# Matrix memory: two gate tiles in the heads' stage, gate steps later; the rotary key's parts in one tile; the first halves' last squares added on VectorE

## The chip, the cores and the metric

The kernel runs on one core of one Trainium2 chip. The metric is the device time of one execution in microseconds (us); lower is better. Three executions of the kernel before took 2184.15, 2185.90 and 2186.45 us, median 2185.9 us.

## What is computed

A trunk of four residual layers over 1024 tokens of 1024 channels: latent attention, a gated MLP with a causal convolution, an mLSTM matrix memory, and a second gated MLP; each is normed (RMS) and modulated by a conditioning vector, and a last norm closes. The parts that matter here:

```
def mla_mixer(h, cos, sin, w_in, q_norm, w_q_up, kv_norm, w_kv_up, w_out):
    proj = h @ w_in                                   # 1024 -> 512 + 256 + 64
    cq, ckv, k_rope = jnp.split(proj, [MLA_Q_LORA, MLA_Q_LORA + MLA_KV_LORA], axis=-1)
    q = (rms_norm(cq, q_norm) @ w_q_up).reshape(B, S, MLA_HEADS, MLA_NOPE + MLA_ROPE)
    k_rope = apply_rope(k_rope, cos, sin)
    kv = (rms_norm(ckv, kv_norm) @ w_kv_up).reshape(B, S, MLA_HEADS, MLA_NOPE + MLA_V)
...
def mlstm_mixer(h, w_in, b_gates, head_norm, w_out):
    proj = h @ w_in
    q, k, v, o, gates = jnp.split(proj, [qk_w, 2 * qk_w, 2 * qk_w + v_w, 2 * qk_w + 2 * v_w], axis=-1)
    def step(carry, inp):                             # one chunk of 64 tokens, per head
        C, n, m = carry
...
        num = (inter_w[..., None] * jnp.einsum('bhvd,bhtd->bhtv', C, qt)
               + jnp.einsum('bhts,bhsv->bhtv', s_mat, vt))
...
        C_new = decay[..., None, None] * C + jnp.einsum('bhs,bhsv,bhsd->bhvd', ws, vt, kt)
        return (C_new, n_new, m_new), h_out
...
    y = hs.reshape(B, S, v_w) * jax.nn.sigmoid(o.astype(jnp.float32))
```

`o` are the output gates, eight tiles of 128 channels.

## The kernel before

**Form of a product.** Tokens lie along the free dimension in two halves of 512 (`hf`), channels along partitions. Each operand is split into a high and a low part in a reduced format (ScalarE copies the high part, VectorE subtracts for the low), and a product is `mm3` (L173): three matmuls of 128x512, high by high, high by low, low by high. The parts `hi` and `lo` of a weight come from `unit` (L164), which loads a raw tile and splits it; the raw tiles of the heads' stage rotate through a small number of buffers, so a load waits for the split of an earlier one. `mm3` also counts down a queue: `later(n, fn, key)` (L188) puts a step after n more calls of `mm3` in the program. Numbers for this stand in a table (L41 to L56). A scheduler then fixes the order on each engine; every engine, and SyncE (SP), which issues the loads and stores, works in that order.

**Start, about 0 to 125 us.** `in_k` (L352) multiplies the k-th 128 channels of both halves with seven weight tiles, for k of 0 to 7, into seven accumulators `ia`. Six tiles are the latent query and key/value; the seventh holds the 64 columns of the rotary key twice (the load is 896 columns wide), since its rotated partner is needed too. After the last k, `evac` (L443) scales the accumulators by the token's norm (`rbs`), `in_norms` (L503) squares and sums them (`ev`), `rstd_cols` (L245) sums over partitions with one-column matmuls (`st`), VectorE and GpSimd make `var` and `rstd`, a transpose spreads it (`rb`), and `norm_gain` (L493) makes `cqn` and `ckvn`, for which the products `qrp`, `kp` and `qp` wait. `rope_key` (L508) adds a bias on ScalarE, and rotates the key.

**Sums of squares.** `Squares.add` (L234) squares a tile on ScalarE and adds it on VectorE; `keep` (L228) squares only, and leaves the tile to the one-column matmuls as a second term. The last tile of a half is kept.

**Products of the memory, about 1126 to 1262 us.** `mixer_products` computes pairs of projection tiles with seven products in place of eight (a scheme after Strassen, over halves of tokens and channels), 4 `mm3` of 128x512 each: four pairs of q and k, two pairs of output gates (`PAIRS`, L88, `OG`, L89). Results go to memory, and the heads' stage loads them again (`ogd`, `qkd`).

**Heads' stage, about 1262 to 1447 us.** First the gate values: `gates0` to `gates3` (L1674 to L1731) are small steps on VectorE, ScalarE and TensorE (`gg`, `gr`, `gp`, `gcol`), put after 2, 18, 22 and 26 `mm3` of `ogates` (L1506), whose matmuls `inp` make the remaining output gates from tile OG on. The rows of the gates are stored (`gd`) and loaded again as rows of all partitions (`crow`, `ib`). Then for each of four heads: `prep` makes scores (`st`), transposed keys (`kp`) and their weighted split (`kw`); `chain` (L1568) runs eight chunks: `pc` is the update of state C, `po` the output from the chunk (`po<-va`) and from C (`po<-C`); `finish` transposes (`yT`). Between the chunks one `mm3` of `ogates` is put (L1764), between the chains the next head's values (`vp`). VectorE's queue holds the dot products of the modulation (`mraw`), the splits and C, in the scheduler's order.

Of the kernel before, what the change touches and what calls it, by code (L numbers as in the profile page):

```python
# [11 lines left out]
F32 = mybir.dt.float32  # L12
# [6 lines left out]
P = 128  # L19
D = 1024  # L20
S = 1024
KT = D // P
HS = 512
NH = 8
# [18 lines left out]
WARM = 14  # L43
W0, W0_RSTD, WF, WF_RSTD = (6, 10), (4, 3), (4, 5), (4, 4)
SHARE = 7
GATES = (2, 18, 22, 26)
MODS = (0,) * 4 + (2,) * 11 + (3,)
# [39 lines left out]
U_MV0 = (U_MV, U_MV + 1, U_MG)  # L87
PAIRS = tuple((U_MQ + i, U_MK + i) for i in range(4)) + ((U_MO, U_MO + 1), (U_MO + 2, U_MO + 3))  # L88
OG = 4  # L89

# [9 lines left out]
def trunk_kernel(ctx: ExitStack, tc: tile.TileContext, xT, pos, c_d, cols_d, mod_w, win, winT, w0, w1, wf, wd, out):  # L100
# [72 lines left out]
    def mm3(ps, ls, rs, first, last, more=False):  # L173

        lh, ll = ls
        rh, rl = rs
        pe.matmul(ps, lh, rh, start=first, stop=False, skip_group_check=more)  # L177
        pe.matmul(ps[:, 0:rl.shape[-1]], lh, rl, start=False, stop=False, skip_group_check=more)  # L178
        pe.matmul(ps, ll, rh, start=False, stop=last, skip_group_check=more)  # L179
        for e in list(queue):  # L180
            e[0] -= 1
            if e[0] == 0:
                queue.remove(e)
                e[1]()


# [131 lines left out]
    sraw = block(4, [P, 4, D], F32, "sraw")  # L318
    wraw = block(5, [P, 4, 896], F32, "wraw")
    us = [[(p0w if k < INNER else p0).tile([P, 896], F32R, name=f"win{j}{k}") for j in "hl"] for k in range(KT)]  # L320

# [14 lines left out]
    def prepare(k):  # L336
        hi, lo = us[k]
        raw = wraw[:, k % 4, :]
        mod_dot(0, 8 + k, sraw[:, k % 4, :])
        mod_bias(0, 8 + k)  # L340
        act.activation(hi, raw, AF.Copy)
        scaled(0, k)
        dve.tensor_tensor(lo, raw, hi.bitcast(F32), ALU.subtract)

# [7 lines left out]
    def in_k(acc, k, hf, then=None):  # L352

        for m in range(7):
            mm3(acc[m], wk(us[k], m), halves(h, hf, k), k == 0, k == KT - 1)
            if then:
                then(m)
# [145 lines left out]
    def in_norms(hf, raw, ev, ps):  # L503

        sq = [Squares(ev, bufs=4), Squares(ev, bufs=4)]
        for m in range(6):
            sq[m // 4].add(raw[:, m, :], bias=inb[:, m:m + 1])
        def rope_key():  # L508
            sl = slice(hf * HS, (hf + 1) * HS)
            t = raw[:, 6, :]  # L510
            act.activation(t, t, AF.Identity, bias=inb[:, 6:7])
            rope_apply(t, raw[:, 7, :], hf)
            act.activation(kkh[:, sl], t, AF.Copy)
            dve.tensor_tensor(kkl[:, sl], t, kkh[:, sl].bitcast(F32), ALU.subtract)

        if hf == 0:
            rope_key()
        cqn[hf] = block(2 + 2 * hf, [P, 2, 4, HS], F32R, "cqn")
        if hf == 0:
            ckvn[0] = block(3, [P, 2, 2, 2, HS], F32R, "ckvn")  # L520

        def gain_q(rb):
            if hf == 1:
                t = p_a[:, 6 * HS:7 * HS]
                act.activation(t, rb, AF.Copy)
                rb = t
            with tc.high_priority():
                norm_gain(raw[:, 0:4], inb[:, 0:4], rb, 4, "qn", cqn[hf][:, 0], cqn[hf][:, 1])

        def gain_kv(rb):  # L530
            if hf == 1:
                t = p_a[:, 7 * HS:8 * HS]
                act.activation(t, rb, AF.Copy)
                rb = t
            norm_gain(raw[:, 4:6], inb[:, 4:6], rb, 2, "kvn", ckvn[0][:, hf, 0], ckvn[0][:, hf, 1])
            if hf == 1:
                rope_key()

        rstd_later(sq[0], 512, cqn[hf], gain_q, EVAC[0], ps)
        rstd_later(sq[1], 256, cqn[hf], gain_kv, EVAC[1], ps)  # L540
# [331 lines left out]
    def out_proj(px, psC, osrc, us, w, l, early=0):  # L872
# [7 lines left out]
        for hf in range(2):  # L880
# [3 lines left out]
            for m in range(KT):  # L884
# [6 lines left out]
                store_x(2 * l, hf, m, x)  # L891
                ssq.keep(x[:, m, :]) if m == KT - 1 else ssq.add(x[:, m, :])
            if hf == 0:
# [76 lines left out]
    def mlp(px, psC, T, l, u_d, pd, done, cols, extra=None, scaled=None, store=None, more=None):  # L970
# [238 lines left out]
        def d_run(i, p, w, t0=0, width=HS):  # L1209
# [14 lines left out]
            if g == len(DG) - 1 and op in ("B22", "T3", "B21", "T4"):  # L1224
                for c0, cw_ in ((0, HS),) if hf == 0 else cols:
                    if t0 <= c0 < t0 + width:
# [3 lines left out]
                        with tc.high_priority():  # L1230
                            if op in ("T3", "T4") and (p == 3 or p == 2 and c0 > 0):
                                stats[hf, c0].keep(xs[hf][:, m, c0:c0 + cw_])
# [272 lines left out]

    def ogates():  # L1506
        for m in range(OG, KT):
            u = unit(w1[U_MO + m])
            for hf in range(2):
# [123 lines left out]
    def run(gen):  # L1633
        while True:
            try:
# [11 lines left out]
                     lambda: pm.tile([P, D], F32, tag="mraw", bufs=MRAWS, name=nm("mraw")), crow2)  # L1647
    va = va_tiles()
    v0 = wp.tile([P, 1024], F32, tag="wraw", bufs=wraws, name=nm("v0"))
    nc.sync.dma_start(v0, va_d)  # L1650
# [82 lines left out]
    for n, gate_step in zip(GATES, (gates0, gates1, gates2, gates3)):  # L1733
        later(n, gate_step, gcol)
    og = ogates()
    piece(og, GATES[3] + 1)
# [8 lines left out]
    for hd in range(MH):  # L1745
# [17 lines left out]
        for _ in chain(hd, pre, va, obs):  # L1763
            piece(og)  # L1764
        ends = lambda hd=hd, obs=obs: finish(hd, obs, 1)
# [56 lines left out]
def arrange(inputs):  # L1822
# [24 lines left out]
    wi = a["mla_w_in"][0]  # L1847
    win = np.concatenate([wi, wi[:, 768:]], axis=1).reshape(KT, P, 896)
    winT = np.ascontiguousarray(win.reshape(D, 896).T).reshape(7, P, D)

# [55 lines left out]
```

## Time and profile before

| | us |
|---|---|
| median of three executions | 2185.9 |
| profiled execution, its own time | 2185.47 |
| its span, first to last instruction | 2183.5 |
| TensorE busy in the span | 2149.2 (98%) |
| VectorE busy | 1746.4 (80%) |
| ScalarE busy | 1076.8 (49%) |
| mean granted TensorE clock | 0.994 |

In the rows of a profile PE is TensorE, PEld its loading of weights, DVE VectorE, ACT ScalarE, POOL GpSimd, SPq the queue of SyncE. A row of instructions gives its start, its length, the engine, the line of the kernel, the operation, the tile written and those read, their shape, how many follow each other, and in brackets the idle time before and what ended it. A row of a stretch gives its ends, its length, then for each engine busy time and (x) instructions, the granted clock of TensorE (1.00 is full), the share of the DMA engines that was busy, and GB/s. Matmuls overlap, so a row's length is not its price: spacing is.

### The profile page before, as it was taken

How to read it: one execution, taken by the hardware profiler on the slowest of the kernel's cores; microseconds unless marked ns; L12 is line 12 of the kernel's file. 1: busy time of each engine (PE TensorE's matmuls, PEld its weight loads, DVE VectorE, ACT ScalarE, POOL GpSimd, SP SyncE). 2: the span in 40 equal slices, each digit the busy share in tenths (PEclk: the TensorE clock that was granted, in tenths of full speed). 3: DMA queues.
4: the chain of work that ended last, by engine and by line, in shares of the span. 5: the costliest groups of instructions: out<-in, count | busy, mean ns of one | idle time of the engine just before them, and what ended most of it. 6: DMA issues, size and time to landing. Idle time of an engine off the chain costs nothing.

```text
span 2183.5 us, 28611 instructions
## 1 busy us (share of the span) xinstructions
PE 2149.2 (98%) x10485; PEld 1804.2 (83%) x10485; DVE 1746.4 (80%) x2789; ACT 1076.8 (49%) x1794; POOL 53.0 (2%) x136
## 2 busy tenths in 40 slices
PE   9999999999999999999999999999999999999998
PEld 7878888787888888878888879988888888887887
DVE  8877778659878777899988458886886777779997
ACT  6465566446544444443365464454554444453335
POOL 0000000000000000000000001000000000000000
PEclk9999999999999999999999999999999999999999
DMA  8412334842443342643143454474143332246212
GB/s 319 151 52 58 98 101 151 272 136 67 160 139 129 127 130 97 204 161 103 51 172 131 142 182 151 147 262 142 59 145 102 111 121 92 78 157 216 68 52 77
DMA packets 120588, 289.89 MB, mean 133 GB/s; under 512 B 13376, under 2 KB 21120, under 8 KB 120448
## 3 DMA queue, kind: packets, MB, share of 16 engines
q1 hardware_dynamic: 120048, 287.68, 40.1%
q8 instruction: 82, 1.34, 0.3%
q14 instruction: 58, 0.48, 0.1%
q10 hardware_dynamic: 400, 0.39, 0.1%
HBM read 233.07 MB, written 52.33 MB: 131 GB/s over the span
## 4 chain that ended last, share of the span: by engine, by line
PE 84%; DVE 7%; DMA 4%; ACT 3%; issue 1%; SPq 1%; POOL 1%; DVEq 0%; POOLq 0%; ACTq 0%
PE pa L179 7%; PE pa L177 7%; PE pa L178 7%; PE pd L179 3%; PE da L177 3%; PE da L178 3%; PE da L179 3%; PE pd L177 3%; PE pd L178 3%; PE sc L675 3%; PE op L177 2%; PE op L179 2%; PE op L178 2%; PE db L179 2%; PE db L177 2%; PE db L178 2%
## 5 line engine op out<-in xcount | busy, mean ns | idle before, releaser
L177 PE MATMUL pa<-T,whi 128*128 128x512 f32 x528 | 205.9, 390 | 0.0
L178 PE MATMUL pa<-T,whi 128*128 128x512 f32 x528 | 205.5, 389 | 0.0
L179 PE MATMUL pa<-T,wlo 128*128 128x512 f32 x528 | 205.1, 389 | 0.0
L993 ACT ACTIVATE whi<-wsum 128x512 fp32r<-128x512 f32 x200 | 121.9, 625 | 145.4 <-PE pa L178 61.5
L994 DVE TENSOR_TENSOR wlo<-wsum,whi 128x512 fp32r<-128x512 f32 x200 | 134.4, 686 | 40.9 <-ACT whi L993 39.6
L993 ACT ACTIVATE whi<-raw 128x512 fp32r<-128x512 f32 x150 | 90.7, 624 | 123.3 <-PE pb L178 61.0
L178 PE MATMUL da<-U,whi 128*128 128x512 f32 (+1 forms) x364 | 139.1, 382 | 0.0
L177 PE MATMUL da<-U,whi 128*128 128x512 f32 (+1 forms) x364 | 139.1, 382 | 0.0
L179 PE MATMUL da<-U,wlo 128*128 128x512 f32 (+1 forms) x364 | 138.7, 382 | 0.0
L994 DVE TENSOR_TENSOR wlo<-raw,whi 128x512 fp32r<-128x512 f32 x150 | 101.6, 686 | 33.2 <-ACT whi L993 33.2
L1197 ACT ACTIVATE whi<-raw 128x1024 fp32r<-128x1024 f32 (+1 forms) x60 | 59.2, 987 | 131.0 <-PE da L178 50.0
L177 PEld LDWEIGHTS pa<-T,whi 128*128 128x128 f32 x528 | 99.1, 188 | 22.4 <-ACT whi L993 1.2
L179 PEld LDWEIGHTS pa<-T,wlo 128*128 128x128 f32 x528 | 99.1, 188 | 20.6
L178 PEld LDWEIGHTS pa<-T,whi 128*128 128x128 f32 x528 | 99.1, 188 | 20.2
L1038 ACT ACTIVATE ct<-a,cols 128x512 f32<-128x512 f32 x88 | 70.8, 809 | 84.1 <-DVE a L1060 47.8
L177 PE MATMUL db<-U,whi 128*128 128x512 f32 x264 | 103.4, 392 | 0.8 <-ACT whi L1197 0.8
L179 PE MATMUL db<-U,wlo 128*128 128x512 f32 x264 | 102.7, 390 | 1.5 <-DVE wlo L1198 1.5
L1148 ACT ACTIVATE U<-q 128x1024 fp32r<-128x1024 f32 x84 | 80.0, 980 | 48.6 <-DVE q L1147 22.8
L178 PE MATMUL db<-U,whi 128*128 128x512 f32 x264 | 102.8, 390 | 0.0
L169 ACT ACTIVATE whi<-wraw 128x1024 fp32r<-128x1024 f32 x58 | 60.9, 1056 | 84.0 <-PE op L178 61.1
L177 PE MATMUL op<-oh,whi 128*128 128x512 f32 x256 | 99.9, 392 | 0.9 <-ACT oh L729 0.9
L178 PE MATMUL op<-ol,whi 128*128 128x512 f32 x256 | 99.6, 390 | 0.0
(432 smaller groups left out, 6176.1 us busy)
## 6 DMA issues: line engine op xcount, KB each, us to landing
raw<-in_wf SPq DMA_DIRECT2D x96, 512.0 KB, 3.9
wraw<-in_w SPq DMA_DIRECT2D x58, 512.0 KB, 3.7
mraw<-in_mod_w SPq DMA_DIRECT2D x56, 512.0 KB, 3.7
ud<-ct SPq DMA_DIRECT2D x88, 256.0 KB, 2.2
q<-ud SPq DMA_DIRECT2D x88, 256.0 KB, 4.7
raw<-in_wd SPq DMA_DIRECT2D x32, 512.0 KB, 3.9
pa<-in_mod_w SPq DMA_DIRECT2D x24, 512.0 KB, 3.6
x<-xd SPq DMA_DIRECT2D x48, 256.0 KB, 4.5
```

The source lines that it names most:

```text
L169: act.activation(hi, raw, AF.Copy)
L177: pe.matmul(ps, lh, rh, start=first, stop=False, skip_group_check=more)
L178: pe.matmul(ps[:, 0:rl.shape[-1]], lh, rl, start=False, stop=False, skip_group_check=more)
L179: pe.matmul(ps, ll, rh, start=False, stop=last, skip_group_check=more)
L675: pe.matmul(ps[:, cs], a[:, qs if n < 3 else qrs_], b[:, cs], start=n == 0, stop=n == 4)
L993: act.activation(hi, src, AF.Copy)
L994: eng.tensor_tensor(lo, src, hi.bitcast(F32), ALU.subtract)
L1038: act.activation(t, a[:, 2:], AF.Identity, bias=col(f"cb{l}", m), scale=cw(m, 2))
L1148: act.activation(hi, w, AF.Copy)
L1197: act.activation(hi, src, AF.Copy)
```

## The change

1. **Rotary key in one tile.** The weights are loaded 832 columns wide, and the low part of the key's 64 columns is written beside its high part, so one tile holds [high | low]. `mm2` does one full matmul with that tile and one with its first 64 columns and the low half of the tokens' values: two in place of three. The accumulator's upper 64 rows are then a part that has to be added; `rope_key` moves the halves past each other with two transfers of 64x512 and adds them and the bias on VectorE, where ScalarE had added the bias.
2. **One pair of output gates less** among the products, and two tiles more in `ogates`, two `mm3` between chunks instead of one; the first of its weights is loaded ahead.
3. **Gate steps** after 2, 20, 24, 28 `mm3`; `rb` of the second half's norm before the memory after 8 instead of 3.
4. **Last squares** of the first half are added on VectorE at both output projections and both MLPs; only the second half's are kept.

```
-W0, W0_RSTD, WF, WF_RSTD = (6, 10), (4, 3), (4, 5), (4, 4)
+W0, W0_RSTD, WF, WF_RSTD = (6, 10), (4, 8), (4, 5), (4, 4)
-GATES = (2, 18, 22, 26)
+GATES = (2, 20, 24, 28)
-PAIRS = tuple((U_MQ + i, U_MK + i) for i in range(4)) + ((U_MO, U_MO + 1), (U_MO + 2, U_MO + 3))
-OG = 4
+PAIRS = tuple((U_MQ + i, U_MK + i) for i in range(4)) + ((U_MO, U_MO + 1),)
+OG = 2
...
+    def mm2(ps, u, rs, first, last):
+
+        rh, rl = rs
+        both = lambda: pe.matmul(ps, u, rh, start=first, stop=last)
+        if first:
+            both()
+        pe.matmul(ps[0:64, :], u[:, 0:64], rl, start=False, stop=False)
+        if not first:
+            both()
+        turns()
...
-        act.activation(hi, raw, AF.Copy)
+        act.activation(hi[:, 0:WIN], raw, AF.Copy)
         scaled(0, k)
-        dve.tensor_tensor(lo, raw, hi.bitcast(F32), ALU.subtract)
+        for o, c0, c1 in ((lo, 0, 768), (hi[:, WIN:896], 768, WIN)):
+            dve.tensor_tensor(o, raw[:, c0:c1], hi[:, c0:c1].bitcast(F32), ALU.subtract)
...
-            t = raw[:, 6, :]
-            act.activation(t, t, AF.Identity, bias=inb[:, 6:7])
-            rope_apply(t, raw[:, 7, :], hf)
+            t, rot = raw[:, 6, :], raw[:, 7, :]
+            for a, b in ((0, 64), (64, 0)):
+                nc.sync.dma_start(rot[a:a + 64, :], t[b:b + 64, :])
+            dve.scalar_tensor_tensor(t, t, inb[:, 6:7], rot, ALU.add, ALU.add)
+            rope_apply(t, rot, hf)
...
-                ssq.keep(x[:, m, :]) if m == KT - 1 else ssq.add(x[:, m, :])
+                ssq.keep(x[:, m, :]) if hf and m == KT - 1 else ssq.add(x[:, m, :])
...
-                            if op in ("T3", "T4") and (p == 3 or p == 2 and c0 > 0):
+                            if op == "T4" and (p == 3 or p == 2 and c0 > 0):
...
-            piece(og)
+            piece(og, 2)
```

TensorE, start, first k: `ia_180` is the seventh accumulator before, `ia_181` with the change, `winh` and `winl` the high and low weights, `h_94` and `h_95` the high and low values. Before:

```order
L177 MATMUL ia_180<-h_94,winh_98 128x512
L178 MATMUL ia_180<-h_95,winh_98 128x512
L179 MATMUL ia_180<-h_94,winl_99 128x512
L177 MATMUL ia_174<-h_94,winh_100 128x512
L178 MATMUL ia_174<-h_95,winh_100 128x512
```

And now:

```order
L194 MATMUL ia_181<-h_94,winh_98 128x512
L197 MATMUL ia_181<-h_95,winh_98 64x512
L178 MATMUL ia_175<-h_94,winh_100 128x512
L179 MATMUL ia_175<-h_95,winh_100 128x512
L180 MATMUL ia_175<-h_94,winl_101 128x512
```

The third matmul is gone, and the second writes 64 rows.

VectorE, end of the start stage: from the additions of the squares of the second half (`ev`) to its gains (`raw<-raw,inb,pa`); `wlo` is a weight's low part, `k` and `q` are splits of products. Before:

```order
L243 TENSOR_TENSOR ev_874<-ev_874 128x512
L607 TENSOR_TENSOR k_938<-kp_939,k_937 128x512
L256 TENSOR_SCALAR var_959<-st_954 128x4
L256 TENSOR_SCALAR var_974<-st_969 128x4
L610 SCALAR_TENSOR_TENSOR q_949<-qp_950,q_948 128x512
L170 TENSOR_TENSOR wlo_1545<-wraw_1542,whi_1544 128x1024
L496 SCALAR_TENSOR_TENSOR raw_843<-raw_843,inb,pa_908 128x512 x3
```

And now:

```order
L630 TENSOR_TENSOR k_932<-kp_933,k_931 128x512
L259 TENSOR_TENSOR ev_868<-ev_868 128x512
L633 SCALAR_TENSOR_TENSOR q_943<-qp_944,q_942 128x512
L272 TENSOR_SCALAR var_953<-st_948 128x4
L272 TENSOR_SCALAR var_968<-st_963 128x4
L534 SCALAR_TENSOR_TENSOR raw_838<-raw_838,inb 128x512
L171 TENSOR_TENSOR wlo_1541<-wraw_1538,whi_1540 128x1024
L517 SCALAR_TENSOR_TENSOR raw_838<-raw_838,inb,pa_902 128x512 x3
```

The key's split now stands ahead of the last addition, the query's split ahead of `var`, and the new addition of the rotary key between `var` and the gains.

VectorE, heads' stage, from `gcol` to the first head's last `kw`. Before:

```order
L1729 COPY gcol<-gcol_11227 128x128
L610 SCALAR_TENSOR_TENSOR kw_11269<-kp_11255,gcol,kw_11268 128x128 x2
L1544 TENSOR_SCALAR crow<-crow,gcol 128x128 x4
L610 SCALAR_TENSOR_TENSOR kw_11269<-kp_11255,gcol,kw_11268 128x128
L1554 TENSOR_TENSOR qT_10934<-qT_10934,ib_11233 128x512
L1544 TENSOR_SCALAR crow<-crow,gcol 128x128
L610 SCALAR_TENSOR_TENSOR kw_11269<-kp_11255,gcol,kw_11268 128x128
L1553 TENSOR_TENSOR crow<-crow,st_11248 128x512
```

And now:

```order
L1757 COPY gcol<-gcol_11076 128x128
L633 SCALAR_TENSOR_TENSOR kw_11118<-kp_11104,gcol,kw_11117 128x128 x3
L1570 TENSOR_SCALAR crow<-crow,gcol 128x128 x4
L171 TENSOR_TENSOR wlo_11817<-wraw_11814,whi_11816 128x1024
L1580 TENSOR_TENSOR qT_10781<-qT_10781,ib_11082 128x512
L1579 TENSOR_TENSOR crow<-crow,st_11097 128x512
L633 SCALAR_TENSOR_TENSOR kw_11118<-kp_11104,gcol,kw_11117 128x128
```

Three of the four `kw` now stand ahead of the rows of the gates, and the fourth behind a weight's split, `qT` and the product with the scores. On TensorE ten `inp` matmuls now stand between the second `kp` and the first `pc`, where none stood; in the later heads six stand between the links of a chain, where three stood.

More of the change, by code (lines that the diff above doesn't have):

```diff
@@ L22 @@
 KT = D // P
+WIN = 832
 HS = 512
@@ L179, in mm3, with turns @@
         pe.matmul(ps, ll, rh, start=False, stop=last, skip_group_check=more)
+        turns()
+    def turns():
         for e in list(queue):
@@ L184, in mm3 @@
                 e[1]()
+    def mm2(ps, u, rs, first, last):
[6 more added lines that the diff above has]
+            both()
+        turns()
     queue = []
@@ L318, in trunk_kernel @@
     sraw = block(4, [P, 4, D], F32, "sraw")
-    wraw = block(5, [P, 4, 896], F32, "wraw")
-    us = [[(p0w if k < INNER else p0).tile([P, 896], F32R, name=f"win{j}{k}") for j in "hl"] for k in range(KT)]
+    wraw = block(5, [P, 4, WIN], F32, "wraw")
+    us = [[(p0w if k < INNER else p0).tile([P, w], F32R, name=f"win{j}{k}") for j, w in (("h", 896), ("l", 768))]
+          for k in range(KT)]
     def load_x(hf, k):
@@ L354, in in_k @@
         for m in range(7):
-            mm3(acc[m], wk(us[k], m), halves(h, hf, k), k == 0, k == KT - 1)
+            if m < 6:
+                mm3(acc[m], wk(us[k], m), halves(h, hf, k), k == 0, k == KT - 1)
+            else:
+                mm2(acc[m], us[k][0][:, 768:896], halves(h, hf, k), k == 0, k == KT - 1)
             if then:
@@ L1506, in ogates @@
     def ogates():
+        u = unit(w1[U_MO + OG])
+        yield
         for m in range(OG, KT):
-            u = unit(w1[U_MO + m])
+            if m > OG:
+                u = unit(w1[U_MO + m])
             for hf in range(2):
@@ L1648, in trunk_kernel @@
     va = va_tiles()
+    og = ogates()
+    next(og)
     v0 = wp.tile([P, 1024], F32, tag="wraw", bufs=wraws, name=nm("v0"))
@@ L1734, in trunk_kernel @@
         later(n, gate_step, gcol)
-    og = ogates()
     piece(og, GATES[3] + 1)
@@ L1847, in arrange @@
     wi = a["mla_w_in"][0]
-    win = np.concatenate([wi, wi[:, 768:]], axis=1).reshape(KT, P, 896)
-    winT = np.ascontiguousarray(win.reshape(D, 896).T).reshape(7, P, D)
+    win = wi.reshape(KT, P, WIN)
+    winT = np.ascontiguousarray(np.concatenate([wi, wi[:, 768:]], axis=1).T).reshape(7, P, D)
     mod_w = np.ascontiguousarray(a["mod_w"].transpose(0, 2, 1)).reshape(2, 48, P, D)
```

## The prediction

> **What bounds the kernel now.** The page first: the span and busy times, then the chain of work that ended last.
>
> ```profile
> span 2183.5 us, 28611 instructions
> PE 2149.2 (98%) x10485; PEld 1804.2 (83%) x10485; DVE 1746.4 (80%) x2789; ACT 1076.8 (49%) x1794; POOL 53.0 (2%) x136
> PE 84%; DVE 7%; DMA 4%; ACT 3%; issue 1%; SPq 1%; POOL 1%; DVEq 0%; POOLq 0%; ACTq 0%
> ```
>
> TensorE is busy 98% of the span and holds 84% of the chain, so the time is nearly matmuls times their spacing, plus the places where TensorE waits. Next the table by stretches, in which I look for the price of one matmul and for the stages that wait.
>
> ```profile
> 50.00:100.00 50.00, 50.00 (x243) 41.24 (x242) 43.42 (x78) 18.68 (x26) 3.03 (x3) 1.00 0.51 168
> 100.00:150.00 50.00, 46.24 (x257) 39.50 (x257) 42.11 (x86) 31.17 (x61) 2.39 (x4) 0.93 0.17 50
> 550.00:600.00 50.00, 50.00 (x222) 41.42 (x221) 44.03 (x72) 25.37 (x43) 0.30 (x3) 1.00 0.49 159
> 1250.00:1300.00 50.00, 45.59 (x253) 38.55 (x251) 23.45 (x58) 27.43 (x48) 4.74 (x9) 0.97 0.67 215
> 1300.00:1350.00 50.00, 49.27 (x374) 46.43 (x373) 43.22 (x110) 28.34 (x80) 6.39 (x9) 1.00 0.50 152
> 1350.00:1400.00 50.00, 48.78 (x369) 45.60 (x368) 40.54 (x106) 25.44 (x68) 5.80 (x9) 1.00 0.54 171
> 1400.00:1450.00 50.00, 47.99 (x345) 43.69 (x344) 43.17 (x99) 30.32 (x70) 3.58 (x4) 1.00 0.53 170
> ```
>
> In 550 to 600 us, pure feed-forward products, 222 matmuls of 128x512 fill 50 us: 0.225 us each, whatever a single row shows (matmuls overlap). TensorE waits in two places: around 100 to 125 us, where the second half's norms end, and in the heads' stage from about 1262 to 1447 us. The waits of TensorE name what for (total, times, longest):
>
> ```profile
> PE rb L264 <- POOL rstd L257: 2.7, 3, 1.3
> PE pc L177 <- DVE kw L610: 2.3, 1, 2.3
> PE kp L177 <- ACT ckvn L497: 1.9, 1, 1.9
> PE inp L177 <- DVE gtok L1658: 1.3, 1, 1.3
> PE yT L1629 <- DVE ob L1622: 1.2, 1, 1.2
> PE po L177 <- DVE C L1585: 1.1, 1, 1.1
> PE gr L1699 <- DVE crow L1695: 0.8, 1, 0.8
> PE po L177 <- ACT C L1588: 0.7, 1, 0.7
> ```
>
> **The change part by part.** The profiled execution took 2185.47 us (span 2183.5); the sum is made against that, and 0.4 us is added to stand against the median, 2185.9. About 0.2% of it, 4.4 us, is what a measurement can tell from no change.
>
> *Sums of squares.* Four sums (first half of both output projections, the T3 end of both feed-forwards) lose their second term. The trace has each of their one-column matmuls twice:
>
> ```profile
> L252 PE MATMUL st<-ones,ev x16: 164/250/250, 102.8 to 104.4; 128*128 128x1 f32 x16
> ```
>
> This row is two sums of four columns, eight matmuls in the program and 16 in the trace; they start 1.6 us apart from first to last, so 0.11 us each. Four sums with 4 columns, 2 entries each, are 32 entries: −3.5 us of TensorE. In place of each stands one VectorE addition of 0.68 us (row below) that the sums now wait for. Between the last product and the sums stand 12, 6 and 4 products of three matmuls: 8.1, 4.1 and 2.7 us, against some 2.1 us for gate, square and addition at 0.7 us each, so it is covered. If not, a sum waits 0.7 us. I take −3.4, bounds −3.5 and −0.7.
>
> *Rotary key.* The key's tile takes two matmuls instead of three, 8 times for each half: 16 × 0.225 = −3.6 us of TensorE. Sixteen of those left fill 64 outputs; no row shows that form. It lies between a one-column matmul's 0.11 and 0.225; it streams the same 512 columns, so I take 0.225. VectorE gets more: with the rows below, 1.21 us for 1024 columns and 0.68 for 512 give 0.15 + 1.04 ns per column, so splitting 768 and 64 apart instead of 896 costs 0.09, eight times 0.7, and two additions of the rotated half cost about 0.7 each: +2.1 us. ScalarE loses two biases. Two small transfers per half are asked for long before their use. What ends the stage?
>
> ```profile
> 101.71 0.68 DVE L243 TENSOR_TENSOR ev<-ev 128x512 f32<-128x512 f32 x1
> ...
> 103.83 0.16 DVE L256 TENSOR_SCALAR var<-st 128x4 f32<-128x4 f32 x1 [0.84 <-PE st L252]
> ...
> 104.81 0.68 DVE L610 SCALAR_TENSOR_TENSOR q<-qp,q 128x512 fp32r<-128x512 f32 x1
> 105.41 1.21 DVE L170 TENSOR_TENSOR wlo<-wraw,whi 128x1024 fp32r<-128x1024 f32 x1
> 106.54 2.07 DVE L496 SCALAR_TENSOR_TENSOR raw<-raw,inb,pa 128x512 f32<-128x512 f32 x3
> ```
>
> VectorE: it is busy 43.42 of the 50 us before 100, and from the evacuations to the gains it runs nearly without a gap; only the sums (0.84 us) make it wait. Behind them the order puts the new addition and a weight split, 0.7 + 1.2, ahead of the gains, where a query split and the weight split stood, 0.7 + 1.2: no difference. So TensorE arrives up to 3.6 us earlier and waits for evacuated tiles, split keys and sums instead, and the later waits (kp 1.9) stay. I gain 0.5 of the 0.84 us; bounds −3.6 (all is had) and +2.1 (all of VectorE's added work is on the path).
>
> *Pair and gates tiles.* In the products 7 × 4 × 3 = 84 matmuls go, in the heads' stage 2 × 2 × 8 × 3 = 96 come: +12 × 0.225 = +2.7 us. VectorE and ScalarE lose about 15 operations in the products, where they don't set the end; they get two weight splits in the heads' stage (1.05 and 1.21 us each), hidden beside some 180 us of TensorE. The last store, for which the first `inp` waits 1.3 us, stays in its place, and so does that wait.
>
> What the 96 do is to lie between the links of the chains: six instead of three from step to step, 3 × 0.225 = 0.7 us more. The wait for C, 1.1, loses 0.7; that for ScalarE's C, 0.7, goes; yT's 1.2 goes, since the second half's transposes now have 6 `inp`, 8 transposes and 16 projection matmuls before them, over 5 us. Sum −2.6; bounds 0 (VectorE, 43 of 50 us here, delays the links again) and −3.2 with the small gaps. The gap of gr, 0.8, goes: the step stands six matmuls, 1.35 us, later.
>
> Then the first pc of head 0. TensorE there, then VectorE, then SyncE's request for the gate rows:
>
> ```profile
> 1292.31 0.60 PE L1558 MATMUL kp<-ident,kT 128*128 128x128 f32 x4
> 1295.17 0.36 PE L177 MATMUL pc<-va,kw 128*128 128x258 f32 x1 [2.26 <-DVE kw L610]
> ```
>
> ```profile
> 1292.43 0.88 DVE L1544 TENSOR_SCALAR crow<-crow,gcol 128x128 f32<-128x128 f32 x4 [2.72 <-DMA crow<-gd]
> ...
> 1293.48 0.68 DVE L1554 TENSOR_TENSOR qT<-qT,ib 128x512 f32<-128x512 f32 x1
> ...
> 1294.68 0.34 DVE L610 SCALAR_TENSOR_TENSOR kw<-kp,gcol,kw 128x128 fp32r<-128x128 f32 x1
> 1294.95 0.67 DVE L1553 TENSOR_TENSOR crow<-crow,st 128x512 f32<-128x512 f32 x1
> ```
>
> ```profile
> 1286.33 0.34 SPq L1534 DMA_DIRECT2D crow<-gd  x1
> ```
>
> pc waits for all four kw, and VectorE works in order: after the second it stands 2.72 us before rows that land at 1292.4, 6.1 us after they were asked for. Now ten `inp` matmuls stand before pc, so TensorE comes at 1292.91 − 0.81 + 10 × 0.225 = 1294.35. But the fourth kw now comes behind four row steps, a weight split, qT and the product with st: 0.88 + 1.21 + 0.68 + 0.67 + 0.34 less some 0.3 of overlap is 3.5 after 1292.4, and pc 0.15 later: 1296.1. Left is a wait of 1.75, and up to 2.2 if the gate rows are stored 0.45 later with their step; it would be 0 if they landed 1.8 us earlier, since one weight load now stands ahead of the stores instead of behind them. I take 1.5: −0.8, bounds 0 and −2.3. Behind that wait stands the clock:
>
> ```profile
> 114.57:121.40 6.83, 5.27 (x14) 4.37 (x15) 5.58 (x14) 5.27 (x11) 0.00 (x0) 0.50 0.38 115
> 1295.58:1298.99 3.41, 3.41 (x12) 2.88 (x11) 3.41 (x10) 2.34 (x6) 0.76 (x1) 0.50 0.79 231
> ```
>
> Right after the wait of 2.26 the granted clock is 0.50 for 3.41 us, which costs 1.7 us; after waits of 1.34 (the first `inp`) and 1.3 (rb) nothing like it. A wait of 1.5 lies between, so half of it: −0.8, bounds 0 and −1.7. The Trainium skill ("TensorE: Matmul & The Clock Gate", What's actually happening) has the clock halved after at least one idle window of about 3.4 us; the lengths here, 3.41 and twice that, are its window, but 2.26 us of idle time were enough, so the measurement decides against that limit; by the page's limit alone no wait of 1.5 to 2.2 would halve it, and the sum would be 0.9 us lower.
>
> *Later row step.* rb of the mixer's norm (its 1.3 us wait) moves behind three more `vf` matmuls, at most 0.225 each: −0.4, bounds 0 and −0.7.
>
> Sum: squares −3.4, rotary −0.5, pair and tiles +2.7, chains −2.6, gr −0.8, pc −0.8, clock −0.8, rb −0.4 = −6.6. 2185.5 − 6.6 = 2178.9 for that execution, 2179.3 against the median.
>
> **The rivals.** *The whole rotary saving is had* (TensorE, not VectorE, paces 90 to 105 us). For it speaks that VectorE waits 0.84 us for the sums there; against it its 87% and the weight splits between the evacuations. 3.1 less: 2176.2. With the pc wait and its clock gone too, 2.4 less again: 2173.8.
>
> *The heads' waits stay.* VectorE is at 86% there, the chain's links stand in its queue behind splits of 1.21 us, and a cover of 0.7 us on TensorE is used up by one of these. Then the chains, pc and the clock give nothing: +4.2, 2183.5, no change by measurement. It is what the count alone gives with gr.
>
> *The clock halves where the norms end.* TensorE's 3.6 us go into waits between 91 and 103 us. If over 2 us of them fall together, the clock halves for one or two windows of 3.41 us, 1.7 or 3.4 lost: 2181.0 to 2182.7. Against it: the added waits stand at four places (evacuation, kp, split of k, sums), about 1 us each. By the page's limit it could not happen.
>
> *Late gate weights: slower.* Each head now uses a whole gate tile instead of a half, through the same two raw buffers, on the queue that also carries the rows. From the load to the split tile:
>
> ```profile
> L169 ACT ACTIVATE whi<-wraw x8: 1042/1050/1062, 1337.8 to 1439.5; 128x1024 fp32r<-128x1024 f32 x8
> DMA to landing us min/median/max: 3.4/4.2/4.8
> ```
>
> 4.2 + 1.05 + 1.21 = 6.5 us from asking. If a load is asked for less than 6.5 us before its first `inp`, TensorE stands there with the whole chain behind it. At 2.5 us late in heads 1 to 3 that is +7.5, on top of the heads' waits that stay (2183.5): 2191.0, slower; it decides from 2.3 us each, where 2190.3 is passed. Against it: no matmul of the heads' stage waits for a weight now, and some 40 us lie between two gate tiles.
>
> **How the numbers follow.** Forecast 0.45 (2179.3, own range 2177 to 2181.5), rotary saving had 0.15, heads' waits stay 0.22, halved clock 0.10, late weights 0.08. The range leaves out the last case, the lowest end of the second and the third's top: 2174.5 to 2186. Faster by over 0.2% means below 2181.5: 0.42 of the forecast, 0.15, and 0.03 of the halved clock, 0.60. Within: 0.03 + 0.22 + 0.07 = 0.32. Slower: 0.08.
>
> **What would show it.** Sums with 8 entries instead of 16 at four places and no wait for an addition before them; between 90 and 105 us more idle time on TensorE and the gains at about 106.5 still; no wait for gr; a wait before the first pc of 1 to 2 us, and at its end the clock row; no C or yT wait in the heads. I am wrong if the gains come 2 us or more earlier (the rotary saving is had), if VectorE's additions make the sums wait, or if `inp` waits for whi or wlo.

## The result, and the profile after

| | before | after |
|---|---|---|
| median of six executions each | 2185.24 us | 2173.49 us |
| lowest and highest | 2183.56, 2186.45 | 2173.03, 2176.36 |
| profiled execution | 2185.47 | 2173.35 |

The ratio is 0.9951, with a 95% interval of 0.9941 to 0.9962: 8.3 to 12.9 us less. It is that of the means; the medians differ by 11.8 us, since four of the six executions after lie between 2173.0 and 2173.7 and two at 2176.3 and 2176.4. The change makes the kernel faster, by 1.6 times the 6.6 us of the forecast's sum after the ratio (10.7 us) and 1.8 times after the medians. The page of the kernel after, span, busy times and chain:

```profile
span 2171.6 us, 28499 instructions
PE 2142.3 (99%) x10449; PEld 1798.6 (83%) x10449; DVE 1742.5 (80%) x2791; ACT 1073.0 (49%) x1787; POOL 54.1 (2%) x136
PE 87%; DVE 6%; DMA 3%; ACT 1%; issue 1%; SPq 1%; POOL 0%; DVEq 0%; POOLq 0%; ACTq 0%
```

TensorE's busy time fell by 6.9 us, its idle time in the span from 34.3 to 29.3. Two stretches of the work are worth a look, cut at the same instructions in both kernels: from the first sums of squares of the tokens to the second half's sums of `ev`, and from the first `inp` to the last `yT`. Before:

```profile
44.17:102.78 58.61, 58.55 (x285) 48.16 (x284) 51.05 (x91) 24.26 (x36) 4.88 (x4) 1.00 0.54 184
1265.60:1447.23 181.63, 174.59 (x1218) 158.51 (x1219) 143.88 (x360) 103.44 (x249) 19.02 (x27) 0.99 0.52 163
```

After:

```profile
42.01:99.94 57.93, 57.16 (x279) 46.13 (x277) 53.05 (x96) 25.11 (x39) 4.34 (x4) 1.00 0.59 199
1240.01:1438.68 198.67, 194.08 (x1314) 176.46 (x1313) 147.31 (x361) 111.88 (x261) 23.31 (x31) 0.99 0.50 159
```

In the first stretch TensorE was busy all the time before (58.55 of 58.61 us) and waits 0.77 us now, while VectorE rose from 87% to 92%. In the second, 96 matmuls came in, and TensorE's idle time fell from 7.04 to 4.59 us. The waits of TensorE after (total, times, longest):

```profile
PE rb L280 <- POOL rstd L273: 2.0, 2, 1.1
PE kp L178 <- ACT ckvn L518: 1.9, 1, 1.9
...
PE pc L178 <- DVE crow L1579: 1.6, 1, 1.6
...
PE po L178 <- DVE C L1611: 1.3, 1, 1.3
PE yT L1655 <- DVE ob L1648: 1.2, 1, 1.2
...
PE sc L698 <- ACT q L632: 0.7, 1, 0.7
...
PE st L268 <- ACT sq L247: 0.6, 1, 0.6
```

The waits of `inp` (1.3), of `gr` (0.8) and of `po` for ScalarE's C (0.7) are gone, that of `pc` is 1.6 in place of 2.3. Those for VectorE's C and of `yT` are still there, though the prediction let them go.

Where the 11.8 us of the two profiled executions came from is read at instructions that both have: their start in the kernel before, and how much earlier (−) or later they come in the others. The last row is how long the clock was halved before 134 us. Each column is one execution.

| us | before | after | rotary alone | vector only | tensor only | squares alone | heads alone | more cover | keys first |
|---|---|---|---|---|---|---|---|---|---|
| first sums of the tokens | 44.17 | −2.15 | −1.76 | +0.06 | −1.72 | −0.51 | −0.79 | −0.90 | −1.32 |
| first `qrp` | 95.98 | −4.53 | −4.15 | +0.19 | −2.33 | −0.77 | −0.70 | −3.35 | −3.77 |
| second half's sums | 102.78 | −2.84 | −2.46 | +0.22 | −0.73 | −0.77 | −0.70 | −1.66 | −2.08 |
| its gains | 106.54 | −2.34 | −2.25 | +0.22 | −0.70 | −0.77 | −0.70 | −1.45 | −1.87 |
| first `pv` | 133.97 | −1.88 | −1.20 | −0.27 | −1.36 | −0.86 | −1.18 | −2.03 | −2.30 |
| clock halved before 134 us | 13.7 | 10.2 | 13.7 | 10.2 | 6.8 | 10.2 | 6.8 | 10.2 | 13.7 |

And from there on, before against after alone: first sums of an output projection 447.65, −3.15; first `pa` 485.33, −4.04; first `da` 903.13, −4.06; first `vf` 1122.43, −4.67; first `ma` 1138.88, −5.03; last `ma` 1254.20, −24.10; first `inp` 1265.60, −25.60; first `pc` 1295.17, −24.83; last `yT` 1447.23, −8.55; last `da` 2171.16, −10.27; end 2183.46, −11.83.

### The profile page after: what moved, and what is told of

The parts are those of the page before. It is cut to its first block, busy times and chain, and to the rows that moved or that the text cites. A ratio compares the mean times of both kernels' runs of the same rounds, so it can differ in the third digit from the quotient of the medians.

```text
span 2171.6 us, 28499 instructions
## 1 busy us (share of the span) xinstructions
PE 2142.3 (99%) x10449; PEld 1798.6 (83%) x10449; DVE 1742.5 (80%) x2791; ACT 1073.0 (49%) x1787; POOL 54.1 (2%) x136
## 4 chain that ended last, share of the span: by engine, by line
PE 87%; DVE 6%; DMA 3%; ACT 1%; issue 1%; SPq 1%; POOL 0%; DVEq 0%; POOLq 0%; ACTq 0%
PE pa L180 7%; PE pa L178 7%; PE pa L179 7%; PE sc L698 3%; PE pd L180 3%; PE da L178 3%; PE da L179 3%; PE da L180 3%; PE pd L178 3%; PE pd L179 3%; PE op L179 2%; PE op L180 2%; PE op L178 2%; PE db L180 2%; PE db L178 2%; PE db L179 2%
```

## The experiments

All times are against runs of the kernel before on the same chip, whose medians were 2184.21 us (each part alone, first run with one more tile), 2185.21 (vector only, tensor only, old gate steps, more cover) and 2183.83 (second run with one more tile, keys first). The ratios are not the quotients of these medians, and differ from them by up to 0.0006. Each "us less" is from the ratio. The theory after the result was: the rotary saving is had in large part, because TensorE and not VectorE paced the stage up to the norms, and the wait of the first `inp`, which was taken to stay, went. The rivals were that VectorE's added work, the clock or the gate steps' place had made the difference.

**Each part alone.** The rotary key's edit alone (its lines are in the diff above, with the loads of 832 columns):

```
+    def mm2(ps, u, rs, first, last):
...
-            mm3(acc[m], wk(us[k], m), halves(h, hf, k), k == 0, k == KT - 1)
+            if m < 6:
+                mm3(acc[m], wk(us[k], m), halves(h, hf, k), k == 0, k == KT - 1)
+            else:
+                mm2(acc[m], us[k][0][:, 768:896], halves(h, hf, k), k == 0, k == KT - 1)
```

> The kernel before with the rotary key's edit alone. Theory P (the prediction's: VectorE sets the end of the start stage, so TensorE's 3.6 us turn into waits): the time falls by 0.5 us or less, and the second half's sums start within 0.5 us of where they were (102.8). Theory R (the rival: the token norm's sums, its row and the evacuations are reached in TensorE's order, and VectorE's work moves with them): the sums start 2.5 to 3 us earlier, at about 100, and the whole falls by 2 to 2.5 us.

Measured: 2181.73 us, 0.9993 [0.9985, 1.0002], 1.5 us less, with an interval from 3.3 less to 0.4 more: by time alone neither theory is ruled out. In its trace (of the slowest of its eleven executions, 2187.09, which lost its time only behind 900 us) the sums come 2.46 earlier, of which some 0.8 is a shorter halved stretch of the clock at the start (the last section), and the first `pv` 1.20. VectorE at the norms:

```profile
102.48 0.75 DVE L534 SCALAR_TENSOR_TENSOR raw<-raw,inb 128x512 f32<-128x512 f32 x1
104.29 2.07 DVE L517 SCALAR_TENSOR_TENSOR raw<-raw,inb,pa 128x512 f32<-128x512 f32 x3
```

The gains stand at 104.29, where they stood at 106.54. In this trace more than the predicted 0.5 us is had, and less than the whole 3.6.

The squares alone:

```
-                ssq.keep(x[:, m, :]) if m == KT - 1 else ssq.add(x[:, m, :])
+                ssq.keep(x[:, m, :]) if hf and m == KT - 1 else ssq.add(x[:, m, :])
...
-                            if op in ("T3", "T4") and (p == 3 or p == 2 and c0 > 0):
+                            if op == "T4" and (p == 3 or p == 2 and c0 > 0):
```

> The kernel before with the four last squares added on VectorE, nothing else. If each place gives what its eight one-column matmuls took (0.89 us), the time falls by 3.5 us and each later row steps 0.9 us down at four places. The other theory, that the added sum makes the one-column matmuls wait, has them wait up to 0.7 us at each place and 0.7 to 2 us in all.

Measured: 2181.24 us, 0.9990 [0.9981, 0.9999], 2.2 us less. The first of the four sums in the kernel before has two terms:

```profile
447.65 0.28 PE L252 MATMUL st<-ones,ssq 128*128 128x1 f32 x2
447.79 0.36 PE L252 MATMUL st<-ones,sq 128*128 128x1 f32 x2
...
449.13 0.36 PE L252 MATMUL st<-ones,sq 128*128 128x1 f32 x2
```

and with the edit one:

```profile
446.03 0.95 PE L252 MATMUL st<-ones,ssq 128*128 128x1 f32 x8
```

From 447.65 to 449.13 and 0.36 is 1.84 us, against 0.95: 0.89 less; the other three places go from 1.84 to 0.95 or 1.02, with no wait of `st` for an addition. In the traces that is 3.5 us in all.

The heads' part alone (two tiles, gate steps, the later `rb`):

```
-PAIRS = tuple((U_MQ + i, U_MK + i) for i in range(4)) + ((U_MO, U_MO + 1), (U_MO + 2, U_MO + 3))
-OG = 4
+PAIRS = tuple((U_MQ + i, U_MK + i) for i in range(4)) + ((U_MO, U_MO + 1),)
+OG = 2
...
-            piece(og)
+            piece(og, 2)
```

> The kernel before with the two gate tiles, the gate steps and the later rb. By the prediction's terms: +2.7 for 12 matmuls more, -2.6 -0.8 -0.8 -0.8 -0.4, so -2.7 us, with the wait before the first inp as before (1.3 us). By the traces of before and of the change: -5 us, since that wait is gone too. The rival that the heads' waits stay has +1.5.

Measured: 2178.94 us, 0.9976 [0.9965, 0.9986], 5.2 us less (3.1 to 7.6). The prediction's terms for these edits make 2.7 less. There is no wait of `inp` either; `pc` and `po` still wait:

```profile
PE pc L177 <- DVE crow L1556: 1.4, 1, 1.4
PE yT L1632 <- DVE ob L1625: 1.2, 1, 1.2
...
PE po L177 <- DVE C L1588: 0.7, 1, 0.7
```

The three parts together take off 0.0041, the whole change 0.0049 within its interval of 0.0038 to 0.0059: they add up as far as can be measured.

**The two sides of the rotary edit.** The edit with a third matmul put back (the second one is done twice, so the low values of the key's tile count twice):

```
-        pe.matmul(ps[0:64, :], u[:, 0:64], rl, start=False, stop=False)
+        for _ in range(2):
+            pe.matmul(ps[0:64, :], u[:, 0:64], rl, start=False, stop=False)
```

> The rotary key's edit with its matmul of 64 columns issued twice, so that the key's tile has three matmuls as before (the result counts that small part twice): VectorE's added work and the transfers without TensorE's saving. Theory P: VectorE's 2.1 us are on the path, up to +2.1 us. Theory R: VectorE follows TensorE with room, so within 0.5 us of the kernel before.

Measured: 2184.28 us, 0.9998 [0.9989, 1.0007], no change. The sums come 0.22 later and `pv` 0.27 earlier: the split in two, the two transfers and the added row step of VectorE cost nothing that shows, and the interval leaves them at most 1.5 us. And the kernel before with two matmuls for the key's tile (the product of its high weights with the low values is left out), nothing else:

```
-        pe.matmul(ps[:, 0:rl.shape[-1]], lh, rl, start=False, stop=False, skip_group_check=more)
+        if n == 3:
+            pe.matmul(ps[:, 0:rl.shape[-1]], lh, rl, start=False, stop=False, skip_group_check=more)
...
-            mm3(acc[m], wk(us[k], m), halves(h, hf, k), k == 0, k == KT - 1)
+            mm3(acc[m], wk(us[k], m), halves(h, hf, k), k == 0, k == KT - 1, n=3 if m < 6 else 2)
```

> The kernel before with two matmuls in place of three for the key's tile, VectorE's work as before (left out: the product of high weights and low values of the rotary key). Theory P: -0.5 us or less, TensorE waits instead. Theory R: the same -2 to -2.5 us as with the whole edit, since VectorE's added work costs nothing.

Measured: 2186.31 us, 1.0005 [0.9995, 1.0015], nothing gained; the interval has room for 1.1 us, so for the predicted 0.5, and none for the 2 of the other theory. It has TensorE's saving, and its sums still come only 0.73 us earlier, as much as in the runs that don't touch this stage (squares alone 0.77, heads alone 0.70). (The −1.36 is that of the first `pv` alone: what stands at 159 us comes only 0.5 earlier in this run, and 1.19 with the heads alone, which has the same halved time.) So no gain from TensorE's saving by itself shows. What became of it stands in the evacuation. VectorE in this run:

```profile
88.91 1.23 DVE L170 TENSOR_TENSOR wlo<-wraw,whi 128x1024 fp32r<-128x1024 f32 x1 [0.50 <-ACT whi L169]
90.05 0.75 DVE L499 SCALAR_TENSOR_TENSOR ckvn<-raw,cols,ckvn 128x512 fp32r<-128x512 f32 x1
90.71 0.74 DVE L497 SCALAR_TENSOR_TENSOR raw<-raw,inb,rb 128x512 f32<-128x512 f32 x1
92.24 0.75 DVE L499 SCALAR_TENSOR_TENSOR ckvn<-raw,cols,ckvn 128x512 fp32r<-128x512 f32 x1 [0.79 <-ACT ckvn L498]
92.91 4.27 DVE L447 TENSOR_TENSOR raw<-ia,rbs 128x512 f32<-128x512 f32 x7
```

and in the kernel after:

```profile
85.93 1.40 DVE L517 SCALAR_TENSOR_TENSOR raw<-raw,inb,rb 128x512 f32<-128x512 f32 x2
87.46 0.75 DVE L519 SCALAR_TENSOR_TENSOR ckvn<-raw,cols,ckvn 128x512 fp32r<-128x512 f32 x1
88.41 1.22 DVE L171 TENSOR_TENSOR wlo<-wraw,whi 128x1024 fp32r<-128x1024 f32 x1 [0.20 <-ACT whi L170]
89.55 3.67 DVE L467 TENSOR_TENSOR raw<-ia,rbs 128x512 f32<-128x512 f32 x6
```

With TensorE's side alone, a weight's split that waits for its high part stands ahead of the first half's last gain, ScalarE's part of that gain comes late, and the second half's evacuation starts at 92.91. In the kernel after both gains stand ahead of the split, and the evacuation starts at 89.55. The link between the two is the token norm of the second half: its `rb` on TensorE stands behind that gain, and waits for it in this run,

```profile
91.60 0.62 PE L265 MATMUL rb<-ident,rstd 128*128 128x128 f32 x4 [0.28 <-DVE raw L497]
```

and the evacuation needs the `rbs` that ScalarE copies from it. In all twelve traces the evacuation starts 2.2 to 3.1 us behind the first half's last gain, which starts at 89.28 in the kernel before, 89.24 in vector only, 90.71 in tensor only, 86.96 in rotary alone and 86.59 in the kernel after. So in the traces the two sides gain nothing apart, and 1 to 2 us together; the timed interval of the two together still includes 0. That the place of these steps on VectorE and ScalarE is the cause fits the rows, but no run moved them alone.

**Why the first `inp` no longer waits.** In the kernel before, ScalarE's split of the first values waited for the last store of the products' results:

```profile
1262.72 1.07 ACT L606 ACTIVATE va<-v 128x1024 fp32r<-128x1024 f32 x1 [6.10 <-DMA ogd<-c]
```

In the kernel after it waits only for its load, and runs while that store is under way (asked for at 1233.29):

```profile
1233.73 1.07 ACT L629 ACTIVATE va<-v 128x1024 fp32r<-128x1024 f32 x1 [1.17 <-DMA v<-vad]
```

The guess was that the result tiles rotate through four buffers, and that with one pair less the last result falls into another one. First the kernel before with one more such tile drawn ahead of all pairs:

```
+                pool.memset(held("raw1", [P, 1024], 4)[:, 0:1], 0.0)
                 v = pD[0].tile([P, 1024], F32, tag="raw1", bufs=4, name=nm("v"))
```

> The kernel before with one more tile taken from the four turning buffers of the products' results (one column of it set to zero on GpSimd, nothing reads it); the order on all engines is otherwise the same row for row. Theory B (the values' tile lies on the buffer of the result that is stored last, and which buffer that is hangs on the number of results taken): the values' split no longer waits for the last store of gate values, the first inp starts about 1.5 us earlier after the value products, and the time falls by 1.3 to 1.5 us. Theory L (the wait went with the change because fewer stores and loads were on the way): no difference, the wait of 1.3 us stays.

Measured: 2185.47 us, 1.0007 [0.9998, 1.0016]. Nothing moved:

```profile
1264.07 1.07 ACT L606 ACTIVATE va<-v 128x1024 fp32r<-128x1024 f32 x1 [5.88 <-DMA ogd<-c]
```

That did not refute the guess. The buffers are not handed out in a fixed turn: by the addresses in the program as built, the last result still lay in the buffer over which the value tile `va` is put. In the kernel after it lies in another one. So the tile was drawn just ahead of the last result, which puts that result where the kernel after has it:

```
+            if g["m"] == 5:
+                pool.memset(held("raw1", [P, 1024], 4)[:, 0:1], 0.0)
             t = held("raw1", [P, 1024], 4)
```

> The kernel before, with one more tile drawn from the buffers of the products' results just ahead of the last result, so that the last stored result lies in the buffer next to the one under the value tile of head 0 and not in that one. In the kernel before and in the run with one more tile drawn earlier (where the last result still fell into the buffer under the value tile), ScalarE's split of the first values waits 5.9 to 6.1 us until the last store has landed, and the first inp waits 1.1 to 1.3. If the buffer that the last result happens to get decides it: that split waits for the load of its values alone (about 1 us), the first inp doesn't wait, first inp 1.1 to 1.5 us earlier, the whole 1 to 2 us shorter, ratio 0.9991 to 0.9996. Rival, the number of pairs and stores decides: the split still waits some 6 us, ratio 1.000.

Measured: 2184.20 us, 0.9996 [0.9987, 1.0005], 0.9 us less by the ratio, 0.4 more by the medians, so no difference in time is shown; but in the trace the wait is gone, and the first `inp` comes 1.35 us earlier, the last `yT` 1.53:

```profile
1256.67 1.05 ACT L606 ACTIVATE va<-v 128x1024 fp32r<-128x1024 f32 x1
```

So the buffer of the last result decides this wait. The number of pairs only happened to change which buffer that is.

**The heads' stage.** The kernel after with the gate steps where they had been:

```
-GATES = (2, 20, 24, 28)
+GATES = (2, 18, 22, 26)
```

> The changed kernel with the gate steps after 2, 18, 22 and 26 as before. By the prediction's terms the wait for gr comes back (+0.8 us) and the first pc waits about as long as in the kernel before (2.3 instead of 1.6, +0.7) with the halved clock behind it (+1.7 if it comes): 0.8 to 3.2 us above the changed kernel. If the added inp matmuls alone cover them: within 0.5 us of it.

Measured: 2174.80 us, 0.9954 [0.9942, 0.9967], against the 0.9951 of the whole change: 0.7 us apart, with intervals that leave some 3 us either way, so neither theory is ruled out by time. In its trace `gr` waits 0.8 again and the first `pc` 1.8, with a halved clock behind it, and the stage from the first `inp` to the last `yT` takes 199.6 us in place of 198.7. The kernel after with one `mm3` between the links of a chain, and the other 32 put ahead of head 0's chain:

```
-            piece(og, 31 - GATES[3])
+            piece(og, 31 - GATES[3] + 32)
...
-            piece(og, 2)
+            piece(og)
```

> The changed kernel with one inp product per chunk instead of two; the other 32 stand before head 0's first chain. The work is the same, only its place differs. If the cover between the links of the chains is what the tiles are for, the waits for C, po and yT come back: +2 to +3 us above the changed kernel (less what a longer stretch before the first pc saves there, up to 1.6). If VectorE delays the links whatever the cover: within 0.5 us.

Measured: 2176.71 us, 0.9961 [0.9947, 0.9974]. The wait of `pc` goes, and those for C come in its place:

```profile
PE po L178 <- DVE C L1611: 3.2, 2, 2.4
```

In the trace the last `yT` comes 4.97 us earlier than before, where the kernel after has 8.55; but 1.6 of these 3.6 us were lost ahead of the first `inp`, where this execution has a halved clock at 1126 us. The stage itself takes 200.6 us in place of 198.7. In these two executions six matmuls between links are worth 1.9 us more than the same ones ahead of the first chain. By the intervals alone the two kernels can't be told apart. Last, the kernel after with the splits of the weighted keys at high priority, in the hope of beating it:

```
+            with tc.high_priority():
+                for c in range(4):
+                    cs = slice(c * P, (c + 1) * P)
+                    split_ps(kw[0][:, cs], kw[1][:, cs], kp[:, cs], gcl(GWS, hd, hf * 4 + c))
```

> The changed kernel, with the weighted keys' splits put at high priority, so that head 0's fourth one stands right behind the four row steps on VectorE, ahead of a weight's split, qT and the product with the scores (2.6 us of VectorE). If the wait of pc (1.64 us) hangs on that place in the queue: pc waits under 0.5 us, the first chain starts 1.2 to 1.6 us earlier, and the time against the kernel before falls from 0.9951 to about 0.9944. Rival, VectorE's work is only put off: the weight's split, pT and C come later by what the keys came earlier, a wait of 1 us or more comes up at the first po or the next inp, and the ratio stays 0.995 or rises to 0.996.

Measured: 2173.52 us, 0.9947 [0.9934, 0.9959], the same as the kernel after. The waits of TensorE:

```profile
PE po L179 <- DVE C L1616: 1.6, 2, 1.0
...
PE pc L178 <- DVE C L1614: 1.2, 1, 1.2
...
PE pc L178 <- ACT kw L632: 0.7, 1, 0.7
```

The first `pc` waits 0.7 instead of 1.6, where under 0.5 was expected, and later links wait for VectorE's C instead. The rival fits: the work on VectorE was put off.

## Why the prediction was right or wrong

It had the direction and most of the mechanisms right, and the size too small: 2179.3 was forecast, 2173.49 came. That median lies below the forecast's own range (2177 to 2181.5) and just below the stated one, 2174.5 to 2186; by the ratio on the 2185.9 it was set against it is 2175.2 (2173.0 to 2177.6), just inside. By its steps:

| step | predicted | between the two profiled executions | that part alone, timed |
|---|---|---|---|
| squares | −3.4 | 4 × −0.89 = −3.6 (3.5 row by row) | −2.2 (−4.2 to −0.2) |
| rotary key, to the first `pv` | −0.5 | −1.9, of which up to 0.8 is the clock | −1.5 (−3.3 to +0.4) |
| pair and gate tiles | +2.7 | −19.07 + 96 × 0.227 = +2.7 | |
| the wait of the first `inp` | 0 | −1.5 | |
| chains, `gr`, `pc`, clock behind it | −5.0 | −4.7 | |
| later `rb` | −0.4 | −0.4 | last four together −5.2 (−7.6 to −3.1) |

The 84 matmuls less among the products took 19.07 us (from 5.03 to 24.10 earlier), so 0.227 each; that price times 96 is 21.8.

**Squares: right**, price and cover.

**Rotary key: the term was mis-sized.** The failing step is "VectorE: ... from the evacuations to the gains it runs nearly without a gap", hence "I gain 0.5". The gap-free run is there, and it takes the same time in both kernels: about 14.4 us from 92.14 to 106.54 before, 14.6 from 89.55 to 104.19 after. But its beginning was taken as fixed, and it moved by 2.6 us. In the kernel before, the first evacuation waits for TensorE, and so does the first square on ScalarE:

```profile
92.14 1.32 DVE L446 TENSOR_TENSOR raw<-ia,rbs 128x512 f32<-128x512 f32 x2 [0.58 <-PE ia L179]
```

```profile
95.95 0.73 ACT L238 ACTIVATE ev<-raw,inb 128x512 f32<-128x512 f32 x1 [1.08 <-PE ia L178]
```

The prediction had a row that speaks for it, 50.00 of 50.00 us busy on TensorE between 50 and 100 us, and read from the same row that VectorE, at 87%, sets the end. TensorE is not the whole of it, though: the `rbs` that the evacuation reads too ends at 91.74, 0.4 us ahead of it,

```profile
91.14 0.60 ACT L401 ACTIVATE rbs<-rb 128x512 f32<-128x512 f32 x1 [0.36 <-PE rb L264]
```

so earlier products alone could have moved the evacuation by 0.4 us. For the rest the first half's last gain had to come earlier, as it does with the whole edit (89.28 to 86.59: two weight splits, 2.35 us, stand between the last two gains before, and nothing after). The order on VectorE, which changed along with the edit, is what the sum had no term for. The price of the second matmul was right: it fills 64 rows and costs what a full one does, 0.24 us from start to start in the kernel after:

```profile
90.98 0.40 PE L197 MATMUL ia<-h,winh 128*64 128x512 f32 x1
91.22 0.39 PE L194 MATMUL ia<-h,winh 128*128 128x512 f32 x1
91.45 0.40 PE L178 MATMUL qrp<-cqn,whi 128*128 128x512 f32 x1
```

Of the 3.6 us of matmuls all is had at the first `qrp` (3.4 to 3.8 in the two runs whose clock at the start was as before), and half of it is given back up to the sums, where TensorE now waits:

```profile
99.11 0.75 PE L698 MATMUL sc<-k,q 128*128 128x256 f32 x4 [0.69 <-ACT q L632]
99.94 1.95 PE L268 MATMUL st<-ones,ev 128*128 128x1 f32 x16
```

So neither the forecast's "−0.5" nor the rival "the whole saving is had" came; the truth is between, at 1 to 2 us. The announced sign, gains 2 us or more earlier, came at 2.34, with up to 0.8 of it from the clock; the two runs whose clock at the start was as before have 1.45 and 1.87.

**The wait of the first `inp`: wrong.** The step is "the last store ... stays in its place, and so does that wait". The store stays; its buffer doesn't, as the runs with one more tile show. 1.5 us.

**Pair and tiles, chains: right in sum, and partly for other places.** Taking each start-to-start spacing over the median of its tile, the delays of TensorE of over 0.5 us between first `inp` and last `yT` fell from 7.7 us in six places to 4.6 in three, the shorter ones, the halved clock among them, by 1.5 in sum; together that is the 4.7 but for 0.1. `gr` and ScalarE's C went as predicted. C of VectorE did not lose 0.7: it was 1.1 and is 1.3, at the same link of the third head (51 of the 84 `pc` stand ahead of it in both kernels). And the `yT` of 1.2 is that of the last head, behind whose chain no further head's work stands. What the prediction didn't count are the many delays under 0.5 us.

**The first `pc`: right.** 1.75 was worked out and 1.5 taken; it waits 1.64, behind the row that was named:

```profile
1266.45 0.88 DVE L1570 TENSOR_SCALAR crow<-crow,gcol 128x128 f32<-128x128 f32 x4 [1.09 <-DMA crow<-gd]
1267.24 1.22 DVE L171 TENSOR_TENSOR wlo<-wraw,whi 128x1024 fp32r<-128x1024 f32 x1
...
1269.60 0.69 DVE L1579 TENSOR_TENSOR crow<-crow,st 128x512 f32<-128x512 f32 x1 [0.53 <-POOL crow L1573]
1270.20 0.35 DVE L633 SCALAR_TENSOR_TENSOR kw<-kp,gcol,kw 128x128 fp32r<-128x128 f32 x1
```

```profile
1270.34 0.39 PE L178 MATMUL pc<-va,kw 128*128 128x258 f32 x1 [1.64 <-DVE crow L1579]
```

The fourth `kw` comes behind the row steps, the weight split, `qT` and the product with the scores, as the order said; one gap of 0.53 for GpSimd was not foreseen.

**The clock: no term of this change.** It is not halved behind `pc` after, but from 2.2 us behind the C wait of 1.27 us:

```profile
1368.35:1371.76 3.41, 3.41 (x13) 2.93 (x13) 2.89 (x8) 1.17 (x4) 0.00 (x0) 0.50 0.81 249
```

One such stretch stands in the heads' stage before and one after, so the difference is nil here; in other runs there are none to two. For the first `pc` alone the runs say more than the forecast's half: its waits of 2.09, 2.16 and 2.26 us (squares alone, rotary alone, the kernel before) all have a halved stretch within 1.2 us behind them, one of 1.81 has and one of 1.94 has not, and of the five between 1.35 and 1.64 none has.

**The rivals.** Late gate weights did not come: no `inp` waits for `whi` or `wlo`. A halved clock where the norms end came: one of 3.41 us begins between 102.0 and 104.3 us in four of the five kernels that have the rotary saving, and in none of the seven others. The halved time before 134 us is still no longer than in the recorded kernel before (the table's last row), because other stretches were shorter in these executions; what the rival cost is not resolved.

**What is left.** The steps make −9.4 of the −11.83. The rest lies where little was edited: between the first `pv` and the first sums at 447 us the difference grows by 1.27, and behind the last `da` by 1.56 (some 0.4 goes the other way elsewhere). The six runs without the whole rotary edit gain 0 to 1.3 there against the same recorded execution, and the second run with one more tile, which edits nothing at the end, gains 0.8 there. Most of it is the spread of executions (six of the kernel before lie 2.9 us apart). Not all: of the 1.27, 0.3 comes up to 359 us, and all six kernels with the rotary key in one tile, vector only among them, gain 0.2 to 0.3 there, while four of the five others gain 0.05 at most and tensor only loses. So this small part seems to belong to the rotary edit. The other 1.0 comes between 359 and 409 us, where the ten other runs gain 0 to 1.4 whatever their edit. The timed parts are 9.0 us together.

## What to carry to other kernels

An engine that runs without gaps sets the end of a stage only from the point at which it starts, so ask for everything that releases its first instruction, here the products on TensorE and a norm's row that hung on VectorE's own earlier work. A matmul saved is had only if the other engines' queues are in an order that can use it; the same saving showed no gain in the kernel where the order stayed unfavourable. And a wait for a store can hang on which buffer the last tile happens to get, so look up whose memory a waiting instruction writes before calling the wait permanent.

## What was not expected of the hardware

The granted clock differs from one execution to the next of the same work. The first halved stretch at the start lasts 6.83 us in the recorded kernel before and 3.41 after:

```profile
8.76:15.59 6.83, 5.70 (x13) 4.13 (x14) 6.47 (x9) 5.29 (x10) 0.00 (x0) 0.50 1.04 373
```

```profile
9.85:13.26 3.41, 2.86 (x8) 2.27 (x8) 3.36 (x7) 2.13 (x4) 0.00 (x0) 0.50 1.05 345
```

Runs that don't touch this stage split the same way: with 3.41 us (squares alone, heads alone) all up to 106 us comes 0.5 to 0.8 us earlier, with 6.83 (both runs with one more tile) within 0.04. The Trainium skill ("TensorE: Matmul & The Clock Gate", What's actually happening) calls the window free-running, so that the number of slow matmuls at the start varies from run to run; these runs agree, with 3.41 and 6.83. The Trainium skill (same page and section) also wants an idle window of about 3.4 us before the clock is halved, and there the measurement decides against it: the halved stretch from 1368.35 us on came after waits of 1.27 and 0.17 us, that at 102.0 after one of 0.69 and shorter ones, with 1.95 us of one-column matmuls among the work between.

Nor does the length of a wait alone decide it. The kernel before and its first variant with one more tile have the same instructions around the second half's `rb`, and the same wait there. Before, with no halved clock behind it:

```profile
1130.35 0.65 PE L264 MATMUL rb<-ident,rstd 128*128 128x128 f32 x4 [1.29 <-POOL rstd L257]
```

The variant, with two halved windows:

```profile
1129.32 1.11 PE L264 MATMUL rb<-ident,rstd 128*128 128x128 f32 x4 [1.29 <-POOL rstd L257]
```

```profile
1128.22:1135.05 6.83, 5.73 (x25) 5.54 (x26) 6.83 (x9) 1.82 (x3) 1.04 (x1) 0.50 0.13 20
```

The wait runs from 1128.03 to 1129.32 and the clock is halved from 1128.22 on, 0.2 us into it, so the wait by itself did not bring it about. The same wait thus goes with a halved clock in one execution and not in another, and the comparison of two single executions carries some us of that.
